# Storing split weights once per stage, and copying both halves of a PSUM bank on ScalarE, in a float32 decoder trunk

## Chip, cores and metric

The kernel runs on one core of a Trainium2 chip. The metric is the device time of one execution in microseconds (us). The engines are named as the profile names them: PE (TensorE), DVE (VectorE), ACT (ScalarE), POOL (GpSimd), and SP (SyncE), whose queue issues nearly all DMAs of this kernel.

## What is computed

A residual stream of 2048 positions by 1024 channels passes two layers, each a mixer followed by a gated per-layer embedding, and a final RMS norm:

```
for i in range(2):
    hn = rms_norm(h, norm_g[i])
    m  = swa_sink_mixer(hn, ...) if i == 0 else rwkv7_mixer(hn, ...)
    h  = h + m
    h  = h + sigmoid(h @ ple_w_gate[i]) * (p[i] @ ple_w_proj[i])
return rms_norm(h, final_norm_g)
```

The first mixer is windowed attention with sinks (16 heads of 64, window 128). The second is RWKV-7: for every head a 64 by 64 state S runs through the 2048 positions,

```
sa = einsum('bhvk,bhk->bhv', S, -kk_t)
S  = S * d_t + outer(sa, kk_t * a_t) + outer(v_t, k_t)
y  = einsum('bhvk,bhk->bhv', S, r_t)
```

and its output is normed, gated with silu(z) and multiplied by `rwkv_w_out`. Everything is float32.

## The kernel before

Activations lie transposed, channels on partitions, in 4 groups `n` of 512 positions (`G`). A float32 product is made of three matmuls in a rounded format: each operand is split into a high part (the rounded value) and a low part (the rest), and `mm3` (L565 to L569) issues high*high, high*low and low*high for each 128 by 128 block of the weight. `split` (L510 to L518) makes the high part on ACT (L516, or L513 with a scale) and the low part on DVE or POOL (L518, or L514 with a scale).

There are four phases: the attention projections (to about 500 us), attention, the RWKV projections (about 1230 to 2000 us), and the RWKV recurrence (to the end). In the second and the fourth a `Dense` object runs beside the main work: it holds a list of jobs (`kind`, `n`), a kind being a weight matrix: `p0`, `p1` or `p` (per-layer projection), `o` (output projection), `g` (gate), `l` (low rank), `z` (RWKV gate projection). A job has 8 units (2 for the projections and for `l`), a unit is 8 steps, and a step is one `mm3`, so 24 matmuls a unit. The main work calls `tick` between its own instructions, and each tick advances Dense by a step. In the attention phase the jobs are p0 for four groups, p1 for two, then `o0 g0 o1 l0 g1 o2 l1 g2 o3 l2 g3`, p1 once more and `l3`; in the recurrence z for four groups, then `o g` for three groups and `p o g` for the last. That makes 86 and 98 units.

`Dense.run` writes the order out by hand. The weight of unit `u` is loaded (`w_load`, L110 to L118) at step 8(u-2), split (`w_split`, L120 to L123) at step 8(u-1)+4 and used from step 8u. So a kind's weights are loaded and split again for every group. The raw tile, the high part `dwh` and the low part `dwl` are 4 KB a partition each and come from one pool of six such slots (`wp`, tag `w4`). A raw load reads 512 KB, in rows of 512 bytes (2 KB for the projections). All loads and stores here are issued by SP, in order. A compiler pass then sets the order of the instructions on each engine; an engine runs its own list strictly in order.

The recurrence works in 32 chunks of 64 positions. `chain` (L1301 to L1336) computes one chunk: the products `r1p`, then `up`, whose two halves of 64 partitions are copied out of one PSUM bank into `uv` (L1320 by DVE, L1321 by ACT), then the state update `sp`, `st` (DVE, L1328), the next chunk's `uv` (DVE, L1331), and the output `y`. `tri` (L1231 to L1285) inverts the triangular matrices that `chain` needs, for four chunks at a time: a recursion of 60 small DVE operations (L1247, L1249), three DVE transposes, and for each chunk two sets of 32 by 32 products in a bank `wq`. Of each, one quarter of the partitions is copied out by ACT and one by DVE (L1272 to `wt`, L1282 to `tt`). `front` prepares a chunk (`aps`, `am`, `bn`), and `output` norms and gates it.

Of the kernel before, what the change touches and what calls it, by code (L numbers as in the profile page):

```python
# [10 lines left out]
F32R = mybir.dt.float32r  # L11
# [7 lines left out]
KT = C // 128  # L19
# [24 lines left out]
def f32(ap):  # L44
    return ap.bitcast(F32)
# [7 lines left out]
class Dense:  # L53
# [54 lines left out]
        return aux  # L108

    def w_load(self, u):  # L110
        kind, n, c = u
        k = self.kinds[kind]
        kt = k.get("kt", KT)
        m = 128 * KT // kt
        raw = self.tr.wp.tile([128, KT * 128], F32, name="wraw", tag="w4")
        w = k["w"][:, k.get("c0", 0) + c * m:k.get("c0", 0) + (c + 1) * m]
        self.nc.sync.dma_start(out=raw.rearrange("p (k m) -> p k m", m=m), in_=w.rearrange("(k p) m -> p k m", p=128))
        return raw  # L118

    def w_split(self, u, raw):  # L120
        hi, lo = (self.tr.wp.tile([128, KT * 128], F32R, name=nm, tag="w4") for nm in ("dwh", "dwl"))
        self.tr.split(hi, lo, raw, scale=self.kinds[u[0]].get("scale"))
        return hi, lo  # L123

    def run(self):
        units, begin, events = [], {}, {}

        def at(step, *what):
            events.setdefault(step, []).append(what)

        owner = []
        for j, (kind, n) in enumerate(self.jobs):
            kt = self.kinds[kind].get("kt", KT)
            b = begin[kind, n] = 8 * len(units)
            units += [(kind, n, c) for c in range(self.kinds[kind].get("units", kt))]
            for k in range(kt):
                free = owner[len(owner) - KT] if len(owner) >= KT else -99
                if "after" in self.kinds[kind]:

                    fill = max(free + 1, begin[self.kinds[kind]["after"], n] + 8 * k + 8)  # L140
                else:
                    fill = max(free, b + k - 9) + 3
                    pre = 3 if "pre" in self.kinds[kind] else 0
                    if pre:
                        at(fill - pre, "pre", j, k)
                    at(fill - pre - self.lead, "fetch", j, k)
                assert fill <= b + k
                at(fill, "fill", j, k)
                if (kind, n) == self.late:
                    at(max(fill, b), "late", j, k)  # L150
                owner.append(8 * len(units) - kt + k)
        for u in range(len(units)):
            at(8 * (u - 2), "w_load", u, None)
            at(8 * (u - 1) + 4, "w_split", u, None)
            for ct in range(KT if "aux" in self.kinds[units[u][0]] and not units[u][2] else 0):
                at(8 * (u + ct) - 4, "aux", units[u][:2], ct)
        raws, tiles, wraw, ws, auxs = {}, {}, {}, {}, {}
        job = -1
        first = -16
        assert first <= min(events)  # L160
        yield
        for s in range(first, 8 * len(units)):
            self.left = 8 * len(units) - s
            for what, a, k in sorted(events.pop(s, []), key=lambda e: ("fetch", "w_load", "fill", "pre", "aux", "w_split", "late").index(e[0])):
                if what == "fetch":
                    kind, n = self.jobs[a]
                    kd = self.kinds[kind]
                    while not kd.get("ready", lambda n, k: True)(n, k):
                        yield
                    raws[a, k] = kd["fetch"](n, k)  # L170
                elif what == "fill":
                    kind, n = self.jobs[a]
                    tiles[a, k] = self.kinds[kind].get("fill", self.fill)(n, k, raws.pop((a, k), None))
                elif what == "pre":
                    kind, n = self.jobs[a]
                    raws[a, k] = self.kinds[kind]["pre"](n, k, raws[a, k])
                elif what == "aux":
                    auxs[a, k] = self.kinds[a[0]]["aux"](a[1], k)
                elif what == "late":
                    while self.rest is None:  # L180
                        yield
                    self.tr.split(*(x[:, G - self.rest.shape[2]:] for x in tiles[a, k]), self.rest[:, k])
                elif what == "w_load":
                    wraw[a] = self.w_load(units[a])
                else:
                    ws[a] = self.w_split(units[a], wraw.pop(a))
            if s >= 0:
                u, i = divmod(s, 8)
                kind, n, c = units[u]
                kd = self.kinds[kind]  # L190
                kt = kd.get("kt", KT)
                k, ct = i % kt, c * (KT // kt) + i // kt
                if k == 0:
                    if ct == 0:
                        job += 1
                    ps = self.mp.tile([128, G], F32, name="ps")
                hi, lo = ws[u]
                m = KT // kt * 128
                sl = slice(k * m + (ct % (KT // kt)) * 128, k * m + (ct % (KT // kt)) * 128 + 128)
                self.tr.mm3(ps, hi[:, sl], lo[:, sl], *tiles[job, k], k == 0, k == kt - 1)  # L200
                if k == kt - 1:
                    self.tr.start(kd["evac"](n, ct, ps, tiles[job, ct] if kt == KT else None, auxs.pop(((kind, n), ct), None)))
                    self.cols_done[kind, n] = ct + 1
            yield
# [225 lines left out]
class Trunk:  # L430
# [712 lines left out]
    def rwkv(self):  # L1143
        nc, ins = self.nc, self.ins
# [8 lines left out]
        with ExitStack() as es:  # L1153
# [28 lines left out]
            half = (slice(0, 64), slice(64, 128))  # L1182
# [48 lines left out]
            def tri(g):  # L1231
# [12 lines left out]
                for r in range(30, 0, -1):  # L1244
                    n = 31 - r
                    t = tmp[:, 0:r * n].rearrange("u (s t) -> u s t", t=n)
# [5 lines left out]
                tt = ttp.tile([128, NP, TG, LC], F32, name="tt")  # L1252
# [9 lines left out]
                for j in range(TG):  # L1262
                    wt = sm.tile([128, NP, 32], F32, name="wt")
                    wq = p_f.tile([128, 2, NP, 32], F32, name="wq", tag="f")
                    for p in range(NP):
                        for e in range(2):
                            r0 = 64 * e
                            nc.tensor.matmul(wq[r0 + 32:r0 + 64, 0, p], lhsT=ag[r0:r0 + 32, p, j, 32:64], rhs=at[r0:r0 + 32, p, j],
                                             start=True, stop=True)
                    for e in range(2):  # L1270
                        cpy = nc.vector.tensor_copy if e else nc.scalar.copy
                        cpy(wt[64 * e + 32:64 * e + 64], wq[64 * e + 32:64 * e + 64, 0])  # L1272
                    yield
                    yield
                    for p in range(NP):
                        for e in range(2):
                            r0 = 64 * e
                            nc.tensor.matmul(wq[r0:r0 + 32, 1, p], lhsT=wt[r0 + 32:r0 + 64, p], rhs=tt[r0 + 32:r0 + 64, p, j, 32:64],
                                             start=True, stop=True)
                    for e in range(2):  # L1280
                        cpy = nc.vector.tensor_copy if e else nc.scalar.copy
                        cpy(tt[64 * e:64 * e + 32, :, j, 32:64], wq[64 * e:64 * e + 32, 1])  # L1282
                    TT[g * TG + j] = tt[:, :, j]
                    yield
                if (g + 1) * TG < NCH:  # L1285
# [15 lines left out]
            def chain(c):  # L1301
                uv, am, tt, bn, xa = UV.pop(c), AM.pop(c), TT.pop(c), BN.pop(c), XA.pop(c)[:, :, :, c % 2]
# [14 lines left out]
                up = p_c.tile([128, NP, 64], F32, name="up", tag="ch")  # L1317
                for p, eo in pairs:
                    mm(up[half[eo], p], lhsT=tt[half[eo], p], rhs=r1[half[eo], p], start=True, stop=True)
                nc.vector.tensor_copy(uv[half[0], 0], up[half[0]])  # L1320
                nc.scalar.copy(uv[half[1], 1], up[half[1]])  # L1321
                self.ticks(STEPS[2])
                if c + 1 < NCH:
                    sp = p_c.tile([128, NP, 64], F32, name="sp", tag="ch")
# [2 lines left out]
                    t = r2.tile([128, NP, 64], F32, name="st")  # L1327
# [52 lines left out]
            load_front(0)  # L1380
            load_ab(0)
            self.start(tri(0))
            self.start(front(0))
            load_front(1)
# [48 lines left out]
```

## Time and profile before

| what | value |
|---|---|
| median of 3 runs | 3120.83 us (3119.34 to 3126.83) |
| profiled execution, its own time | 3124.84 us |
| its span, first to last instruction | 3123.0 us |
| granted PE clock, mean | 0.961 of full speed |
| PE busy | 2885.0 us (92%) |
| DVE busy | 2112.2 us (68%) |
| ACT busy | 1438.3 us (46%) |
| DMA moved | 532.87 MB |

All durations that stand in rows come from the one profiled execution. Its own time is 1.8 us above its span and 4.0 us above the median of the runs. A row of the windows view gives a stretch, its length, the busy time and instruction count of each engine, then the granted PE clock as a share of full speed (2.4 GHz; the lower level is 1.2 GHz), the busy share of the 16 DMA engines, and GB/s.

### The profile page before, as it was taken

Reading aid. Unit: us, or ns where it says so; the run is one execution under the profiler, and the core shown is the slowest. Engines: PE = TensorE matmul, PEld = TensorE weight load, DVE = VectorE, ACT = ScalarE, POOL = GpSimd, SP = SyncE. Lnnn points to the kernel's source line nnn. Section 1 sums busy time; section 2 is a strip of 40 time slices with the busy share of each in tenths; the row PEclk is TensorE's granted clock in tenths of the full one; section 3 lists DMA queues with packets and bytes.
Section 4 is the critical chain, followed back from the end, with each engine's and each line's share of the span. In section 5 each row is a group of like instructions: output and inputs, shape, how many; then the busy total and the mean of one; then the engine's idle time right before and its main releaser. Section 6 shows DMA issues by size and latency. Waiting matters only on the chain. (4 is left out here: it accounts for less than half of the span.)

```text
span 3123.0 us, 56427 instructions
## 1 busy us (share of the span) xinstructions
PE 2885.0 (92%) x21416; PEld 2284.2 (73%) x21416; DVE 2112.2 (68%) x3665; ACT 1438.3 (46%) x2976; POOL 1023.5 (33%) x886
## 2 busy tenths in 40 slices
PE   7999998999999988898999899988989988989997
PEld 5888886777777766686777688766767766767876
DVE  6532434775888766738678966688795686795555
ACT  5311115874675644626667733433334443443433
POOL 2243500002211232404556700214454435435421
PEclk9999999999999999999999899998899999999999
DMA  7665847985675455636556778855657558568463
GB/s 220 184 142 110 172 131 207 248 210 151 170 189 143 145 172 172 194 115 190 180 185 199 214 210 218 236 150 145 145 150 176 126 143 202 116 150 204 122 192 95
DMA packets 704032, 532.87 MB, mean 171 GB/s; under 512 B 255504, under 2 KB 558736, under 8 KB 703760
## 3 DMA queue, kind: packets, MB, share of 16 engines
q1 hardware_dynamic: 696080, 518.76, 60.3%
q0 software_dynamic: 7680, 10.50, 3.1%
q8 instruction: 169, 2.77, 0.4%
q14 instruction: 103, 0.84, 0.1%
HBM read 350.09 MB, written 168.56 MB: 166 GB/s over the span
## 5 line engine op out<-in xcount | busy, mean ns | idle before, releaser
L567 PE MATMUL ps<-dhi,dwh 128*128 128x512 f32 x1472 | 609.8, 416 | 17.0 <-ACT dwh L516 11.7
L569 PE MATMUL ps<-dhi,dwl 128*128 128x512 f32 x1472 | 595.2, 405 | 26.7 <-DVE dwl L518 15.0
L568 PE MATMUL ps<-dlo,dwh 128*128 128x512 f32 x1472 | 594.3, 405 | 8.3 <-DVE dlo L518 6.1
L567 PE MATMUL ps<-xH,wh 128*128 128x512 f32 x1408 | 556.9, 402 | 25.4 <-DVE kb L1049 10.5
L568 PE MATMUL ps<-xL,wh 128*128 128x512 f32 x1408 | 560.7, 399 | 1.8 <-DVE xL L518 1.1
L569 PE MATMUL ps<-xH,wl 128*128 128x512 f32 x1408 | 561.5, 399 | 0.8 <-DVE wl L518 0.8
L569 PEld LDWEIGHTS ps<-dhi,dwl 128*128 128x128 f32 x1472 | 283.2, 192 | 96.0 <-DVE dwl L518 18.9
L567 PEld LDWEIGHTS ps<-dhi,dwh 128*128 128x128 f32 x1472 | 283.0, 192 | 88.1 <-ACT dwh L516 12.7
L567 PEld LDWEIGHTS ps<-xH,wh 128*128 128x128 f32 x1408 | 269.4, 192 | 88.9 <-DVE kb L1049 14.0
L568 PEld LDWEIGHTS ps<-dlo,dwh 128*128 128x128 f32 x1472 | 283.5, 193 | 67.8 <-DVE dlo L518 8.4
L568 PEld LDWEIGHTS ps<-xL,wh 128*128 128x128 f32 x1408 | 270.8, 192 | 62.3 <-DVE xL L518 2.3
L569 PEld LDWEIGHTS ps<-xH,wl 128*128 128x128 f32 x1408 | 269.9, 192 | 59.3 <-DVE wl L518 1.7
L518 DVE TENSOR_TENSOR dwl<-wraw,dwh 128x1024 fp32r<-128x1024 f32 x152 | 193.8, 1275 | 106.4 <-ACT dwh L516 99.9
L516 ACT ACTIVATE dwh<-wraw 128x1024 fp32r<-128x1024 f32 x152 | 160.5, 1057 | 195.8 <-PE ps L568 122.4
L677 POOL DMA_DIRECT2D t<-t x160 | 126.2, 1272 | 200.2 <-DVE t L674 107.1
L851 ACT ACTIVATE S<-S,nm 128x256 f32<-128x256 f32 (+1 forms) x256 | 125.6, 494 | 65.5 <-DVE nm L848 60.1
L516 ACT ACTIVATE wh<-wr 128x1024 fp32r<-128x1024 f32 x44 | 46.6, 1060 | 188.3 <-DMA wr<-in_attn_w_in 142.9
L518 POOL TENSOR_TENSOR xL<-xs,xH 128x512 fp32r<-128x512 f32 x72 | 111.1, 1554 | 67.7 <-ACT xH L516 67.0
L1247 DVE TENSOR_TENSOR tmp<-P 128x30 f32<-128x30 f32 (+14 forms) x240 | 114.1, 476 | 11.2 <-POOL P L1238 5.2
L842 DVE CUSTOM_DVE_ANT_0 S<-sc,mask,sink 128x256 f32<-128x256 f32 (+1 forms) x256 | 109.0, 469 | 17.6 <-PE sc L838 17.5
L953 DVE SCALAR_TENSOR_TENSOR xs<-hp,mu,xs 128x512 f32<-128x512 f32 x96 | 95.3, 1004 | 29.5 <-ACT xs L952 29.1
L1249 DVE TENSOR_TENSOR P<-P,tmp 128x30 f32<-128x30 f32 (+14 forms) x240 | 110.1, 459 | 6.5
(258 smaller groups left out, 5341.6 us busy)
## 6 DMA issues: line engine op xcount, KB each, us to landing
wraw<-in_ple_w_gate SPq DMA_DIRECT2D x64, 512.0 KB, 4.3
hp<-hn SPq DMA_DIRECT2D x72, 256.5 KB, 4.0
sz<-th SPq DMA_DIRECT2D x64, 256.0 KB, 4.3
ple<-pt SPq DMA_DIRECT2D x64, 256.0 KB, 5.9
wraw<-in_attn_w_out SPq DMA_DIRECT2D x32, 512.0 KB, 4.4
aux<-ple SPq DMA_DIRECT2D x64, 256.0 KB, 3.9
yd<-kx SPq DMA_DIRECT2D x32, 512.0 KB, 4.5
wraw<-in_rwkv_w_in SPq DMA_DIRECT2D x32, 512.0 KB, 4.8
```

What stands on the lines that cost most here:

```text
L516: nc.scalar.activation(hi, src, AF.Copy)
L518: e.tensor_tensor(out=lo, in0=src, in1=f32(hi), op=ALU.subtract)
L567: mm(ps, lhsT=wh, rhs=ah, start=first, stop=False)
L568: mm(ps, lhsT=wh, rhs=al, start=False, stop=False)
L569: mm(ps, lhsT=wl, rhs=ah, start=False, stop=last)
L677: nc.gpsimd.dma_start(out=t1[32 * d:32 * d + 32, :], in_=t2[32 * a:32 * a + 32, :], accum_op=ALU.add)
L842: nc.vector.tensor_tensor_reduce(out=S[:, i, c0:], in0=sc[:, eo, c0:], in1=mask[:, c0:], scale=1.0, scalar=sink[:, 4 * g + 2 * j + eo:4 * ...
L851: nc.scalar.activation(S[:, i, c0:], S[:, i, c0:], AF.Exp, bias=nm[:, i:i + 1], accum_out=den[:, i:i + 1])
L953: nc.vector.scalar_tensor_tensor(out=src, in0=t[:, :G], scalar=mus[:, c, k:k + 1], in1=src, op0=ALU.mult, op1=ALU.add)
L1247: nc.vector.tensor_tensor(out=t, in0=P[:, 0:r, r:r + 1].broadcast_to([128, r, n]), in1=P[:, r:r + 1, r + 1:].broadcast_to([128, r, n]), op ...
L1249: nc.vector.tensor_tensor(out=P[:, 0:r, r + 1:], in0=P[:, 0:r, r + 1:], in1=t, op=ALU.add)
```

## The change

There are two edits.

First, `Dense.run` notes for every kind the group of its first job (`first`) and whether it comes again (`again`). A unit of the first group is loaded and split as before; if the kind comes again, the two parts are also stored to a scratch tensor in DRAM (`parts`, 2 by 512 KB for a unit). A unit of a later group loads both parts from there into two slots (`w_parts`), at the step at which it loaded the raw weight, and nothing is split. The rows of these transfers are 4 KB, one a partition.

Second, the copies at L1272, L1282, L1320 and L1321 are all made by ACT.

```
     def w_load(self, u):
         kind, n, c = u
         k = self.kinds[kind]
+        if n != self.first[kind]:
+            return self.w_parts(u)
...
+    def w_parts(self, u):
+        hl = tuple(self.tr.wp.tile([128, KT * 128], F32R, name=nm, tag="w4") for nm in ("dwh", "dwl"))
+        for a, t in enumerate(hl):
+            self.nc.sync.dma_start(out=f32(t), in_=self.parts(u)[a])
+        return hl
+
+    def parts(self, u):
+        return self.tr.dram(f"wp_{self.name}{u[0]}{u[2]}", [2, 128, KT * 128])
+
     def w_split(self, u, raw):
+        if u[1] != self.first[u[0]]:
+            return raw
         hi, lo = (self.tr.wp.tile([128, KT * 128], F32R, name=nm, tag="w4") for nm in ("dwh", "dwl"))
         self.tr.split(hi, lo, raw, scale=self.kinds[u[0]].get("scale"))
+        if self.again[u[0]]:
+            for a, t in enumerate((hi, lo)):
+                self.nc.sync.dma_start(out=self.parts(u)[a], in_=f32(t))
         return hi, lo

     def run(self):
         units, begin, events = [], {}, {}
+        self.first, self.again = {}, {}
+        for kind, n in self.jobs:
+            self.again[kind] = kind in self.first
+            self.first.setdefault(kind, n)
...
                     for e in range(2):
-                        cpy = nc.vector.tensor_copy if e else nc.scalar.copy
-                        cpy(wt[64 * e + 32:64 * e + 64], wq[64 * e + 32:64 * e + 64, 0])
+                        nc.scalar.copy(wt[64 * e + 32:64 * e + 64], wq[64 * e + 32:64 * e + 64, 0])
...
                     for e in range(2):
-                        cpy = nc.vector.tensor_copy if e else nc.scalar.copy
-                        cpy(tt[64 * e:64 * e + 32, :, j, 32:64], wq[64 * e:64 * e + 32, 1])
+                        nc.scalar.copy(tt[64 * e:64 * e + 32, :, j, 32:64], wq[64 * e:64 * e + 32, 1])
...
-                nc.vector.tensor_copy(uv[half[0], 0], up[half[0]])
-                nc.scalar.copy(uv[half[1], 1], up[half[1]])
+                for eo in range(2):
+                    nc.scalar.copy(uv[half[eo], eo], up[half[eo]])
```

## Rows read from the trace of the kernel before

**Rows 1.** The page: busy time of each engine, and PE's granted clock in 40 slices.
```profile
PE 2885.0 (92%) x21416; PEld 2284.2 (73%) x21416; DVE 2112.2 (68%) x3665; ACT 1438.3 (46%) x2976; POOL 1023.5 (33%) x886
PEclk9999999999999999999999899998899999999999
```

**Rows 2.** Windows: the recurrence, one of eight stretches in it, all eight summed.
```profile
2050.00:3000.00 950.00, 857.79 (x11156) 680.96 (x11155) 715.55 (x1078) 384.52 (x801) 428.57 (x350) 0.95 0.63 152
...
2100.00:2170.00 70.00, 57.66 (x749) 45.92 (x743) 68.13 (x105) 23.60 (x41) 38.88 (x32) 0.88 0.42 106
...
sum 410.00, PE 340.35 PEld 268.93 DVE 395.93 ACT 143.76 POOL 177.66; mean PE 42.54 PEld 33.62 DVE 49.49 ACT 17.97 POOL 22.21
```

**Rows 3.** Waits of PE, 2050 to 3123 us: us in total, times, longest.
```profile
PE y L1334 <- DVE uv L1320: 15.6, 7, 4.9
...
PE ps L569 <- DVE dwl L514: 11.7, 4, 4.9
PE aps L1208 <- DVE tt L1282: 10.1, 4, 3.3
PE ps L569 <- DVE dwl L518: 8.0, 5, 3.3
```

**Rows 4.** Timeline of 2136 to 2152 us: start, us, engine, line, [idle before <-releaser].
```profile
2138.35 0.52 PE L1319 MATMUL up<-r,tt 64*64 64x64 f32 x12
...
2142.16 2.06 DVE L518 TENSOR_TENSOR dwl<-wraw,dwh 128x1024 fp32r<-128x1024 f32 x1
...
2144.27 0.50 PE L569 MATMUL ps<-dhi,dwl 128*128 128x512 f32 x1 [3.33 <-DVE dwl L518]
...
2146.31 0.67 DVE L1320 COPY uv<-up 64x512 f32<-64x512 f32 x1
...
2147.02 0.58 ACT L1321 COPY uv<-up 64x512 f32<-64x512 f32 x1 [9.24 <-DVE uv L1320]
```

**Rows 5.** Costliest groups: weight splits of all phases; then the scaled ones, from 2050 us.
```profile
L518 DVE TENSOR_TENSOR dwl<-wraw,dwh 128x1024 fp32r<-128x1024 f32 x152 | 193.8, 1275 | 106.4 <-ACT dwh L516 99.9
L516 ACT ACTIVATE dwh<-wraw 128x1024 fp32r<-128x1024 f32 x152 | 160.5, 1057 | 195.8 <-PE ps L568 122.4
...
L514 DVE SCALAR_TENSOR_TENSOR dwl<-wraw,dwh 128x1024 fp32r<-128x1024 f32 x32 | 41.8, 1305 | 12.1 <-ACT dwh L513 11.9 <-DMA uv<-vn 0.2
```

**Rows 6.** Single lines: copies with ns min/median/max; last, one of ACT's waits, 2050 to 3050 us.
```profile
L1272 DVE COPY wt<-wq x32: 429/429/432, 2077.2 to 2865.6; 32x256 f32<-32x256 f32 x32
...
L1282 ACT COPY tt<-wq x32: 343/362/362, 2082.2 to 2870.1; 32x256 f32<-32x256 f32 x32
...
L1320 DVE COPY uv<-up x32: 646/679/683, 2089.8 to 2973.8; 64x512 f32<-64x512 f32 x32
...
L1321 ACT COPY uv<-up x32: 581/581/583, 2090.6 to 2974.5; 64x512 f32<-64x512 f32 x32
...
ACT uv L1321 <- DVE uv L1320: 121.7, 28, 14.3
```

**Rows 7.** The eight stretches, instructions of `dwl` alone (PE, PEld, DVE); last, L1320 alone.
```profile
2400.00:2440.00 40.00, 11.48 (x30) 5.60 (x29) 3.66 (x3) 0.96 0.52 116
2510.00:2570.00 60.00, 14.84 (x36) 6.87 (x36) 6.12 (x5) 0.97 0.60 141
...
sum 410.00, PE 98.11 PEld 46.42 DVE 37.80; mean PE 12.26 PEld 5.80 DVE 4.73
...
sum 410.00, DVE 8.78; mean DVE 1.10
```

**Rows 8.** DMA issues: count, KB each, median us to landing; then a window of dense work alone.
```profile
wraw<-in_ple_w_gate SPq DMA_DIRECT2D x64, 512.0 KB, 4.3
...
yd<-kx SPq DMA_DIRECT2D x32, 512.0 KB, 4.5
...
3020.00:3090.00 70.00, 68.45 (x300) 54.80 (x299) 34.64 (x41) 24.97 (x58) 6.48 (x4) 1.00 0.41 125
```

**Rows 9.** Line L117, the weight loads: their time to landing, min/median/max.
```profile
DMA to landing us min/median/max: 3.5/4.6/13.4
```

## Prediction

> **What bounds the kernel now.** I read the page's busy times first. PE is busy 92% of the span, DVE 68%, ACT 46% [rows 1]. The change leaves the matmuls alone, so it can give back only the time in which PE stands still (3123.0 - 2885.0 = 238 us) and the time in which it runs at the lower clock. The 40 slices show where the clock falls: at the start, around 550, 650, 1100 to 1500, 1750, and again and again after 2050 us. The next view is therefore the windows of the recurrence. From 2050 to 3000 us PE is idle 950 - 857.8 = 92.2 us, and the mean clock is 0.95 [rows 2]. Eight stretches of 20 to 70 us, 410 us together, hold 410 - 340.4 = 69.7 us of these 92; in them DVE is busy 395.9 us, that is 97% [rows 2]. These are the stretches in which the recursion of `tri` runs. So in 43% of this phase DVE is the bound, and PE the bound in the rest.
>
> Third, the waits of PE say which DVE results are late: `uv` of L1320 15.6 us, `dwl` of L514 11.7 and of L518 8.0, `tt` of L1282 10.1 [rows 3]. All four are instructions that the change removes from DVE, wholly or in most units; together 45.4 us.
>
> Fourth, the timeline of one such place shows how. The products `up` end about 2138.9 us. Their copy L1320 starts on DVE only at 2146.3, since DVE works off recursion steps and a 2.06 us `dwl` first; PE waits 3.33 us for that `dwl`, and ACT stands 9.24 us before its own half, L1321 [rows 4]. The last point matters: ACT's copy reads other partitions than DVE's, yet it starts only when DVE's has ended. ACT loses 121.7 us in 28 such waits [rows 6]. The program orders the two readers of one bank.
>
> **Part one: weights kept as parts.** Of 86 units in the attention phase, 22 are of a first group (p0 2, p1 2, o 8, g 8, l 2), and of 98 in the recurrence 26 (z 8, p 2, o 8, g 8). So 136 units lose their split. 24 of these are scaled ones (o in the recurrence, groups 1 to 3), 112 are plain. DVE loses 112 x 1.275 + 24 x 1.305 = 174 us and ACT 136 x 1.057 = 144 us [rows 5].
>
> Outside the DVE-bound stretches this lies beside PE work and is worth nothing but the waits it ends. In the eight stretches `dwl` costs DVE 37.8 us. Two of them are first passes, which keep their split: 2400 to 2440 is o0 (3.7 us), 2510 to 2570 nearly all g0 (6.1) [rows 7]. That leaves 28.0 us that DVE loses where it is the bound.
>
> What is added: 136 x 2 = 272 loads for 136, and 46 units of the first groups that come again (22 + 24; p of the recurrence is used once) store 2 x 512 KB each. So SP issues 228 more DMAs, and 136 x 0.52 + 46 x 1.05 = 119 MB more are moved. One transfer of 512 KB lands in the same time whether its rows are 512 bytes (the gate's weights, 4.3 us) or 4 KB (yd, a store of the very shape of a part, 4.5 us) [rows 8]. In a window of dense work alone the DMA engines move 125 GB/s at a busy share of 0.41, so about 305 GB/s at full share [rows 8]; 119 MB is then an estimate of 390 us of their time, 12% of the span. It is hidden where their share is below 0.85; the mean in the recurrence is 0.63 [rows 2].
>
> Is a part there in time? A part's slot comes free with the last matmul of unit u-3, and unit u begins two units later: 48 matmuls. In the window of dense work PE did 300 in 68.45 us, so 48 take 11.0 us at the least, against 4.6 us to landing in the median and 13.4 at worst [rows 8, 9]. The stores wait on SP for the split of their own unit; behind them on SP stand the loads of the next chunk and of the next weights. The loads of raw weights wait there today for the same splits, so I take the queue at nothing, with up to +13 us for one full landing [rows 9] that a crowded start of the attention phase may push onto PE. I take +3: nearer to nothing, since two p0 units are stored before the crowd.
>
> One cost sits in the slots. Where a first-group unit is followed by a later-group one, the pool of six must hold the running unit's two, the raw tile, the next unit's two parts loaded early, and two more for the split: seven. The low part waits for the running unit's last matmul. There are seven such places (after p0, p1, g0, l0 in the attention phase; after z0, o0 g0, and the late p). The price is between 0 and one ACT and one DVE split, 1.06 + 1.28 = 2.3 us [rows 5]: 0 to 16 us together. I take +4, since the high part still finds a slot and PE needs the low part only in a unit's third matmul.
>
> **Part two: copies on ACT.** DVE loses 32 x 0.679 = 21.7 us (L1320), 32 x 0.429 = 13.7 (L1272) and about as much at L1282; ACT gains 32 x (0.581 + 2 x 0.362) = 42 us [rows 6], less than the 144 us it loses. In the eight stretches it is L1320 that counts, 8.8 us [rows 7]. On the chain itself the two halves take 0.68 + 0.58 = 1.26 us one after the other today and 2 x 0.58 = 1.16 on ACT: nothing. The gain is that no half waits behind the recursion. What is queued behind them on ACT are `dwh`, `am` and `th`; they stood 121.7 us behind L1321 and now wait for 0.58 us more of work.
>
> The Trainium skill speaks against this edit: "PSUM — Partial Sum Buffer", section "PSUM bank collisions raise a hardware error", says that two engines may read one bank at once when they are in different 32-partition quadrants, as these halves are. Had the copies run so, one engine for both would add 32 x 0.58 = 18.6 us to the chain, and the sum below would be some 27 us instead of 46. The trace does not show them so: in rows 4 ACT's copy stands behind DVE's, after 9.24 us of waiting; the sum goes by the row.
>
> **The sum.** (a) DVE-bound stretches: 28.0 + 8.8 = 36.8 us less DVE work, under the 69.7 us that PE is idle there, so -36.8. (b) Outside them, `tt` of L1282: between 0 and -10.1 [rows 3]; -6, because ACT has room. (c) The clock: 950 x 0.05 = 47.5 us of work lost at most [rows 2], between 0 and all of it. It falls behind PE's idle time, and (a) and (b) take nearly half of that, but in a DVE-bound stretch a faster PE only waits longer; -10. (d) slots +4, (e) DMA +3. Sum -45.8 us. From the profiled execution's 3124.84 us this gives 3079.0; against the median of 3120.83, 4.0 lower, **3075**. Its own bounds: (a) may be half as large or half as large again (18 to 55 us), (c) may reach half of the clock (24 us); together they move the sum by some 28 us either way, 3047 to 3103.
>
> **Rivals.**
>
> The relief goes deeper (chance 0.10). If three quarters of the 92.2 idle us and of the 47.5 us of clock go, 105 us, less the +7 of (d) and (e): about 3023. For it speaks that all four waits named end; against, that the recursion stays on DVE and goes on meeting POOL's work.
>
> The freed DVE time is filled again (0.17). DVE instructions are stretched when POOL works beside them: a `dwl` of 1.2 us took 2.06 in rows 4. The recursion may stretch into the room, or another late result may take the place of `dwl`. Then only the direct order gains: a quarter of (a) and (b), -11, with -3 of clock and +7: -7, about 3114. The Trainium skill has the rule for it, "SBUF — State Buffer", section "SBUF: two separate sides": DVE with two SBUF inputs and GpSimd share a port pair that one locks for its whole instruction. A `dwl` is such an instruction and its removal also frees POOL, so by the rule this rival should be weak.
>
> Weights come late (0.10, slower). The place is dense work with nothing between: the end of the attention phase and the last 16 units. The point is where a part's landing passes the 11.0 us lead. The worst landing today, 13.4 us [rows 9], would stop PE 2.4 us a unit, and with twice the bytes behind one another 4.5 us is not absurd: 16 units at the end and some 22 of the attention tail, 38 x 2.4 = 91 us at the worst, 75 as the case that decides. With the gain that is 3075 + 75 = 3150. Against it: the DMA share there is only 0.41 [rows 8].
>
> The change does what it says on the page, so a rival of no effect is the second one.
>
> **Numbers.** Forecast 0.63, deeper 0.10, filled 0.17, late 0.10. About 0.3% (9.4 us) is what a measurement of this kernel can tell from no change. Faster by more than that: nearly all of the forecast (0.61), deeper 0.10, and a part of filled (0.07), 0.78. Within it: 0.11. Slower: the late weights and an edge of others, 0.11. The range goes from 3035, into the deeper case, to 3118, over most of the filled one.
>
> **What would show it.** Right: DVE busy falls by about 220 us and ACT by about 100; 48 weight splits are left; the waits for `dwl` and L1320 nearly go; in the `tri` stretches PE's busy share rises from 83% and the clock with it; ACT no longer waits for DVE at L1321. Wrong: DVE still 97% busy over as many us (filled); PE waits for DMA of `dwh` (late); PE waits on `dwl` at the seven places for more than 2 us each (slots); a new wait behind ACT's copies. What would upset the sum most is that the compiler pass orders each engine's list anew, which the trace of before can't show.

## The result, and the profile after

The changed kernel takes **3078.73 us** (median of 4 runs, 3062.65 to 3083.21) against 3120.9 (median of 4, 3119.34 to 3126.83): a ratio of **0.985, 95% interval 0.982 to 0.988**, or 42 us. The forecast was 3075, with a range of 3035 to 3118. The total is right to 4 us; where the 42 us come from is mostly not where the forecast had them. In the experiments below, the ratios leave out two executions of the kernel before that took 5463 and 11877 us.

The profiled execution took 3082.86 us, with a span of 3081.1. First the page's busy times, and the weight splits that are left (two lines of the view of single source lines: ns min/median/max, first and last start).

```profile
PE 2863.4 (93%) x21416; PEld 2265.3 (74%) x21416; DVE 1907.0 (62%) x3433; ACT 1356.3 (44%) x2936; POOL 1002.1 (33%) x886
PEclk9999999999999999999999999998999999999999
...
DMA packets 622689, 652.42 MB, mean 212 GB/s; under 512 B 259153, under 2 KB 433361, under 8 KB 622417
...
L540 DVE TENSOR_TENSOR dwl<-wraw,dwh x40: 1180/1224/1823, 468.8 to 2962.7; 128x1024 fp32r<-128x1024 f32 x40
L536 DVE SCALAR_TENSOR_TENSOR dwl<-wraw,dwh x8: 1212/1218/1503, 2334.9 to 2424.8; 128x1024 fp32r<-128x1024 f32 x8
```

Against [rows 1], DVE loses 205 us and ACT 82. 40 plain splits are left here and 8 scaled ones on L536, 48 together. The DMAs move 119.6 MB more. The work changed as the diff says. Of the three slices with an 8 in the clock's row one is left.

Now the recurrence in the windows view, a window of the same length, 42 us earlier (columns as explained with the profile before), and then one place of the recursion in it.

```profile
2008.00:2958.00 950.00, 868.26 (x11230) 685.43 (x11230) 625.16 (x959) 379.91 (x849) 421.39 (x353) 0.95 0.76 211
...
2130.00:2180.00 50.00, 40.80 (x422) 31.94 (x419) 48.81 (x74) 17.81 (x32) 33.36 (x26) 0.83 0.64 178
...
sum 340.00, PE 288.96 PEld 229.42 DVE 322.16 ACT 113.33 POOL 146.23; mean PE 41.28 PEld 32.77 DVE 46.02 ACT 16.19 POOL 20.89
```

Against [rows 2], DVE is relieved of 90 us (715.55 to 625.16), but PE's idle time falls only from 92.2 to 81.7 us, and the clock stays at 0.95. The last line is the sum of seven stretches of 30 to 60 us in which DVE is still about 95% busy; before there were eight, 410 us long. PE is idle 51.0 us in them (69.7 before), and outside them 30.7 (22.5 before). The edges of these stretches are set by eye and the new ones are 70 us shorter in all, so the split between inside and outside is rough. The whole is not: from the first `r1p` to the last `y`, the same work in both kernels, DVE is busy 106 us less (729.1 before, 623.3 now), and PE is idle only 7.5 us less (93.0 and 85.5). PE's busy time is 869.15 us in both.

PE's waits from 2008 us to the end (us in total, times, longest) name what is late now:

```profile
PE ps L589 <- ACT dhi L538: 14.4, 7, 9.2
PE ps L421 <- DVE th L327: 14.2, 7, 7.1
PE r1p L1327 <- DVE uv L1351: 12.0, 4, 6.1
PE ps L591 <- DVE dwl L540: 11.2, 4, 6.7
PE wq L1290 <- DVE at L1277: 6.3, 1, 6.3
...
PE r1p L1327 <- POOL tt L1282: 5.1, 2, 2.7
PE ps L591 <- DVE dwl L536: 4.8, 1, 4.8
...
PE ps L591 <- DMA dwl<-wp_wo: 0.3, 1, 0.3
```

Compare [rows 3]. The wait for `uv` of L1320 (15.6 us) is gone, and there stands one for the chain's next DVE step, `uv` of L1351 (L1331 before), with 12.0. `dwl` fell from 19.7 us (11.7 and 8.0) only to 16.0, though most of its instructions are gone. At the top stands a wait that ACT seems to cause.

The timeline of that place shows what it is (start, us, engine, line, [idle before <-releaser]):

```profile
2140.93 1.76 DVE L299 SCALAR_TENSOR_TENSOR xs<-xs,mu,raw 128x512 f32<-128x512 f32 x1
2142.61 1.47 DVE L1269 TENSOR_TENSOR tmp<-P 128x220 f32<-128x220 f32 x1
...
2150.33 1.12 DVE L1269 TENSOR_TENSOR tmp<-P 128x238 f32<-128x238 f32 x1
...
2153.70 0.41 DVE L1269 TENSOR_TENSOR tmp<-P 128x238 f32<-128x238 f32 x1
...
2154.90 0.75 DVE L299 SCALAR_TENSOR_TENSOR xs<-xs,mu,raw 128x512 f32<-128x512 f32 x1
...
2155.74 0.63 ACT L538 ACTIVATE dhi<-xs 128x512 fp32r<-128x512 f32 x1 [12.33 <-DVE xs L299]
...
2156.43 0.80 PE L589 MATMUL ps<-dhi,dwh 128*128 128x512 f32 x1 [9.20 <-ACT dhi L538]
```

PE waits 9.20 us for ACT, but ACT itself waited 12.33 us for `xs`, a single DVE instruction of 0.75 us. Between this `xs` and the one before it, DVE works off 15 instructions of the recursion in one piece, 12.3 us. Nothing of what the change removed is in this piece. That is the mechanism that most of these waits share: **DVE runs its list in order, and a long piece of recursion in the list holds up whatever stands behind it.** Take out `dwl` and `uv`, and `xs`, `th` or the next `uv` stands there.

The piece is long for a second reason. Its first eight instructions, with POOL at work beside them, take 1.1 to 1.5 us each, and the later ones, with POOL idle, 0.4 us: about 5 of the 12.3 us. Over the phase this adds up. The first of the eight groups, with POOL idle beside it, needs 19.9 us of DVE for its 60 instructions; the other seven need 26 to 33. At 19.9 us for each group, an estimate, some 64 of the recursion's 223 us would go. No run takes POOL's work away, so what that is worth to PE is not shown.

**Where the 42 us arise.** The first matmul of two lines and the last of a third cut each trace in four parts: the first low-rank product `ls` ends the attention phase, the first `r1p` and the last `y` bound the recurrence. All numbers are from one profiled execution each, in us, with the difference to the kernel before.

| kernel | to first `ls` | to first `r1p` | to last `y` | to the end |
|---|---|---|---|---|
| before | 1252.8 | 765.9 | 961.9 | 142.4 |
| after | 1222.5 (-30.3) | 761.9 (-4.0) | 954.4 (-7.5) | 142.3 |
| the same again, other chip | 1221.6 (-31.2) | 755.7 (-10.2) | 943.2 (-18.7) | 142.4 |

The second part, the RWKV projections, is the same in all kernels, and yet differs by up to 10 us; differences of that size in one profile are no evidence. 30 us in the first part are: they come back, as 26 to 31, in every run that has the whole first edit there, and the three other kernels without it end that part within 5 us of the kernel before. The prediction had no gain in that part.

Two places make up most of it. In the windows view, kernel before and then after:

```profile
600.00:800.00 200.00, 194.35 (x1032) 151.57 (x1031) 137.51 (x361) 126.16 (x324) 29.52 (x20) 0.98 0.69 190
1040.00:1260.00 220.00, 198.00 (x842) 156.03 (x841) 148.46 (x184) 108.51 (x179) 67.77 (x55) 0.95 0.55 168
```

```profile
600.00:800.00 200.00, 200.00 (x1070) 156.02 (x1069) 136.19 (x369) 124.14 (x320) 32.68 (x21) 1.00 0.98 312
1040.00:1260.00 220.00, 206.15 (x881) 162.88 (x880) 126.70 (x157) 96.60 (x159) 78.34 (x68) 0.98 0.76 250
```

The first stretch loses its 5.7 us of idle time and gets the full clock; in the second 13.9 of 22.0 idle us are left and the clock rises from 0.95 to 0.98. That is 38 and 39 matmuls more in the same time. Counted by PE's matmuls, the kernel after is 2.6 us ahead where the kernel before stands at 650 us, 13.8 at 700, 11.5 at 1100 and 29.3 at 1250: about 11 us come from the first place and 18 from the tail. What stood there in the kernel before, in its timeline, first the place near 690 us and then the phase's tail:

```profile
678.62 0.73 SPq L117 DMA_DIRECT2D wraw<-in_attn_w_out  x1
...
692.12 1.06 ACT L516 ACTIVATE dwh<-wraw 128x1024 fp32r<-128x1024 f32 x1 [7.40 <-DMA wraw<-in_attn_w_out]
...
693.23 0.80 PE L567 MATMUL ps<-dhi,dwh 128*128 128x512 f32 x1 [5.03 <-ACT dwh L516]
```

```profile
1102.09 0.72 ACT L952 ACTIVATE xs<-hp,omu 128x512 f32<-128x512 f32 x1 [2.52 <-DMA hp<-hn]
1104.62 0.72 ACT L952 ACTIVATE xs<-hp,omu 128x512 f32<-128x512 f32 x1 [1.80 <-DMA hp<-hn]
...
1107.67 1.04 ACT L516 ACTIVATE dwh<-wraw 128x1024 fp32r<-128x1024 f32 x1
...
1108.77 0.80 PE L567 MATMUL ps<-dhi,dwh 128*128 128x512 f32 x1 [6.20 <-ACT dwh L516]
1111.73 0.80 PE L569 MATMUL ps<-dhi,dwl 128*128 128x512 f32 x1 [1.74 <-DVE dwl L518]
...
1127.62 0.50 PE L569 MATMUL ps<-dhi,dwl 128*128 128x512 f32 x1 [3.03 <-DVE dwl L518]
```

The load issued at 678.62 is the one that took the 13.4 us of [rows 9]; its split, and PE behind it, waited for it. This is a load of `o0`, a first group, which the kernel after loads and splits as well. So what stood here is not what the change takes out. From 670 to 695 us PE stands idle 4 to 5 us in the traces of all four kernels whose attention phase is as before, and not at all in any trace with the edit there; in the kernel after, no load of this stretch takes over 10.3 us to land. Why none comes as late as in the kernel before, among more transfers, is not shown.

In the tail it is the order again: ACT's list has the first mixes of the next phase (`xs`, L952) ahead of a weight split, and these wait for their input from DRAM, while the split's own tile is there. PE stands 6.20 us, then works at the lower of its two levels for about 6 us (0.63 us a matmul, against 0.39 ahead of the stall). These are units of later groups. In the kernel after they have nothing on ACT and DVE, so nothing of theirs can stand behind anything there.

### The profile page after: what moved, and what is told of

Read it like the earlier page. It is cut to its first block, busy times and chain, and to the rows that moved or that the text cites. A ratio compares the mean times of both kernels' runs of the same rounds, so it can differ in the third digit from the quotient of the medians.

```text
span 3081.1 us, 56458 instructions
## 1 busy us (share of the span) xinstructions
PE 2863.4 (93%) x21416; PEld 2265.3 (74%) x21416; DVE 1907.0 (62%) x3433; ACT 1356.3 (44%) x2936; POOL 1002.1 (33%) x886
## 5 line engine op out<-in xcount | busy, mean ns | idle before, releaser
L591 PE MATMUL ps<-dhi,dwl 128*128 128x512 f32 x1472 | 593.5, 404 | 16.8 <-DVE dwl L540 11.5
L1269 DVE TENSOR_TENSOR tmp<-P 128x30 f32<-128x30 f32 (+14 forms) x240 | 113.0, 471 | 16.1 <-POOL P L1260 9.7
L1052 POOL TENSOR_TENSOR kb<-kb,mhalf 128x16 f32<-128x16 f32 x32 | 100.6, 3146 | 33.8 <-DVE kb L1051 33.3
L264 DVE TENSOR_TENSOR aux<-ps,aux 128x512 f32<-128x512 f32 x64 | 43.8, 686 | 108.3 <-PE ps L591 95.7
L1233 ACT COPY am<-aps 128x512 f32<-128x512 f32 x128 | 69.5, 591 | 90.5 <-PE aps L1230 90.1
```

The source lines that it names most:

```text
L591: mm(ps, lhsT=wl, rhs=ah, start=False, stop=last)
L1052: nc.gpsimd.tensor_tensor(out=bs[:, :, 0], in0=bs[:, :, 0], in1=self.mhalf.broadcast_to([128, m]), op=ALU.pow)
L1233: nc.scalar.copy(am[:, 4 * i:4 * i + 4, eo], pse[eo])
L1269: nc.vector.tensor_tensor(out=t, in0=P[:, 0:r, r:r + 1].broadcast_to([128, r, n]), in1=P[:, r:r + 1, r + 1:].broadcast_to([128, r, n]), op ...
```

## The experiments

All ratios are against runs of the kernel before on the same chip, with their 95% interval. The table goes on with the parts of the one above.

| kernel | time, us | ratio | to `ls` | to `r1p` | to last `y` |
|---|---|---|---|---|---|
| copies_only | 3104.99 | 0.995 (0.993 to 0.997) | +1.0 | -0.6 | -17.1 |
| att_weights | 3095.93 | 0.993 (0.990 to 0.996) | -31.1 | -1.8 | +5.1 |
| rec_weights | 3095.64 | 0.993 (0.991 to 0.995) | +4.3 | -8.5 | -17.9 |
| weights_only | 3067.05 | 0.983 (0.980 to 0.986) | -28.9 | -10.2 | -16.7 |
| change_again | 3071.21 | 0.984 (0.982 to 0.987) | -31.2 | -10.2 | -18.7 |
| weights_uv | 3069.93 | 0.984 (0.982 to 0.986) | -28.9 | -7.9 | -22.5 |
| no_recursion | 3003.07 | 0.963 (0.960 to 0.965) | -29.4 | -6.4 | -84.7 |
| slow_recursion | 3052.16 | 0.979 (0.976 to 0.981) | -30.2 | -4.1 | -39.5 |
| att_last_group | 3114.55 | 0.9984 (0.9974 to 0.9995) | -14.8 | -0.6 | +3.1 |
| before_slow | 3121.29 | 1.000 (0.999 to 1.001) | +1.2 | -8.9 | +0.4 |
| weights_slow | 3070.01 | 0.985 (0.981 to 0.989) | -26.2 | -7.0 | -23.4 |
| early_slow | 3088.61 | 0.990 (0.988 to 0.992) | -29.6 | -8.8 | +13.6 |

**The second edit alone** (copies_only): the kernel before with the four copies on ACT.

```diff
-                nc.vector.tensor_copy(uv[half[0], 0], up[half[0]])
-                nc.scalar.copy(uv[half[1], 1], up[half[1]])
+                for eo in range(2):
+                    nc.scalar.copy(uv[half[eo], eo], up[half[eo]])
```

(and the same for `wt` and `tt`.)

> The kernel before with the copies at L1272, L1282, L1320 and L1321 on ScalarE; weights as before. First theory (the prediction's: VectorE's room in the stretches of the recursion is what counts): about 9 us of VectorE work leave those stretches and the wait for uv of L1320 ends, so 9 to 15 us faster, all of it after 2000 us. Second theory (from the two traces: the attention phase gave most of the gain, by weights no longer split behind other work): 0 to 5 us faster, since VectorE takes up the room again. Both: nothing changes before 2000 us beyond 3 us.

Measured: 14 us faster, 17 in the recurrence of its profile. PE's and ACT's waits from 2010 us on:

```profile
PE r1p L1305 <- DVE uv L1329: 27.1, 8, 6.2
...
ACT uv L1319 <- PE up L1317: 20.3, 20, 1.6
```

ACT's wait for DVE (121.7 us, [rows 6]) is gone, and so is PE's for the copy (15.6 us, [rows 3]). The chain's next DVE instruction has taken it over with 27.1 (4.6 in the kernel before). Both halves on one engine did not make the kernel longer. The rule of the Trainium skill that the prediction weighed ("PSUM — Partial Sum Buffer", section "PSUM bank collisions raise a hardware error": engines in different quadrants may read a bank at once) would by the prediction's estimate have put 18.6 us onto the chain; in this kernel the program orders the two copies, and the measurement decides. The two copies share the bank that they read and also the tile that they write; which of the two makes the program order them, no run shows.

**The first edit in one phase only** (att_weights, rec_weights): `kept` takes the place of the test on `first`.

```diff
+    def kept(self, kind, n):
+        return n != self.first[kind] and (self.name == "a")
```

(in rec_weights the name is "w".)

> The change's first edit in the attention phase alone (weights of the recurrence are split for every group as before, and no copy is moved). First theory: between +7 and -5 us, as the sum had it (slots and DMA cost about what the end of the phase gains). Second theory: 25 to 32 us faster, 11 of them near 690 us and 18 between 1090 and 1230 us, where the kernel before waits for weight splits; PE's waits for dwh and dwl between 600 and 1250 us go from about 16 us to under 3.

> The change's first edit in the recurrence alone, no copy moved. First theory: 28 us of splits leave the stretches in which VectorE is busy 97%, with some of the clock 30 to 38 us faster. Second theory: at most 10 us faster; PE's idle time in the 950 us of the recurrence falls from 92 us to no less than 80, and waits for other VectorE results take the place of those for dwl.

Measured: 23 us faster with either. In att_weights the whole gain stands ahead of the first `ls` (-31.1), as in the change; the recurrence gives none of it (+5.1, within what single profiles differ by). So the attention phase is worth 23 to 31 us by itself, though PE was 90% busy there and more. In rec_weights the first part shows no gain, and the recurrence gains 18, with `PE y <- DVE uv` still at 15.9 us. So neither phase alone is the cause; the prediction's place is half of it at the most.

**The first edit alone, and the change again** (weights_only, change_again).

> The change's first edit in both phases, no copy moved. First theory: 37 us of the 46, so about 3084 us. Second theory: the sum of the two phases, 30 to 40 us faster. If the parts add up, this is att_weights and rec_weights together within 5 us, and the changed kernel less copies_only.

> The changed kernel itself, beside runs of the kernel before on this chip, so that it can be set beside the parts. The earlier runs give 0.985 for it and 0.983 for its first edit alone; the two edits alone took 13.6 and 51.6 us. If the edits added up it would be 65 us faster than before, 0.979; if both only empty the same queue, 40 to 50 us, 0.984 to 0.987.

The first edit alone is 52 us faster; its two phases alone gave 23 each, 46 together, so within the intervals they add. The change is 49 us faster in its second measurement, 42 in its first. So the copies do not add: worth 14 us alone, they are worth nothing that can be measured beside the weights (0.984 and 0.985 with them, 0.983 without). PE's waits in weights_only from 1980 us:

```profile
PE y L1356 <- DVE uv L1342: 16.1, 7, 5.2
PE ps L591 <- DVE dwl L540: 14.5, 5, 6.4
```

The wait for the copy is there as before (16.1 us), so it is no longer worth its own size: what ends it brings up another wait. The runs of the change spread from 3062.65 to 3083.21 us over both measurements; the two profiles differ mostly in the recurrence, 954.4 against 943.2 us.

**Only the copy of the chain** (weights_uv): the first edit, and of the copies only `uv` on ACT.

> The first edit in both phases, and of the copies only L1320 (uv) on ScalarE; wt and tt as before. If the uv copy is what counts of the second edit (PE waits 16 us for it in the first edit alone), this is 10 to 16 us faster than the first edit alone, 0.978 to 0.980. If the wait only moves on to the next VectorE step of the chain (L1331, uv of the next chunk) it is within 6 us of the first edit alone, and PE's wait for that step rises from 2.5 us to over 10.

3069.93 us, the same as weights_only. The wait for the copy goes, and this one comes:

```profile
PE r1p L1329 <- DVE uv L1353: 10.0, 4, 3.9
```

It was 2.5 us in weights_only. The wait moved one DVE instruction on along the chain. The other two copies (`wt`, `tt`) are not what spends the gain.

**Taking the recursion away** (no_recursion): the change, with the last 2 of the 30 recursion steps; 56 of the 60 DVE instructions of a group are left out, so the inverse is not computed.

```diff
-                for r in range(30, 0, -1):
+                for r in range(2, 0, -1):
```

> The changed kernel with the triangular recursion cut to its last two of 30 steps (56 of 60 VectorE operations of each of the 8 groups left out, some 205 us of VectorE work in all; the inverses are not formed). If the recursion's run of VectorE work is what holds PE in the recurrence, PE's idle time between 2000 and 2960 us falls from 82 to under 35 us, and the kernel is 50 us or more faster than the changed one. If the stops come from elsewhere (the chain's own latency, PSUM, DMA), PE stays idle for over 60 us and less than 25 us are gained.

The recurrence loses 85 us against before, 66 to 77 more than the change. The windows of the recurrence, this kernel and then change_again:

```profile
1980.00:2940.00 960.00, 927.86 (x11586) 736.44 (x11587) 477.86 (x562) 396.30 (x880) 445.92 (x366) 0.97 0.83 234
```

```profile
1980.00:2940.00 960.00, 876.88 (x11329) 691.32 (x11327) 637.63 (x988) 384.11 (x855) 423.23 (x356) 0.96 0.77 215
```

PE's idle time falls from 83 to 32 us. Everything else is in place: the weights' DMAs, the copies, the chain. So in the changed kernel the recursion on DVE is what holds PE in this phase. The kernel before was not run without it. Leaving the recursion out also makes the inverse ready sooner, but PE's waits for the inverse itself are small in the list of the kernel after: 6.3 us for `at` and 5.1 for `tt`, of 85.5 idle. Most of the waits there are for other results on DVE or behind it.

**Spreading the recursion** (slow_recursion): the change, and in the program the recursion gives way to other work after every step instead of every second. No work is left out.

```diff
-                    if r % 2:
-                        yield
+                    yield
```

> The changed kernel with one yield after every step of the recursion instead of after every second, so that its 60 VectorE operations are spread over twice as many ticks of the main loop (same work). If it is the density of these runs that makes PE wait, VectorE's stretches over 95% get thinner and the kernel is 10 to 30 us faster than the changed one. If the compiler's order packs them anyway, or the inverse now comes late to its chunk, it is within 6 us or slower.

**3052.16 us** (3049.64 to 3058.74), ratio 0.979 (0.976 to 0.981): 19 us faster than the change on the same chip and 68 than the kernel before, the best of those that form the inverse. PE's waits from 1980 us:

```profile
PE ps L591 <- DVE dwl L540: 15.7, 4, 7.2
PE ps L421 <- DVE th L327: 9.6, 8, 3.4
```

The chain's wait for `uv` is down to 1.9 us, from 9.9 in change_again. But the trace does not show the recursion in shorter pieces. In DVE's timeline 19 pieces of it run for over 5 us with no other instruction between, 138 us together; in change_again there are 17, 130 us together. From first to last instruction the eight groups take 295 us instead of 327, with fewer other instructions between, and 209 us of DVE instead of 225. The largest difference is in the third group, here the stretch around it in change_again and then in slow_recursion:

```profile
2114.00:2166.00 52.00, 42.04 (x426) 32.16 (x425) 50.09 (x84) 17.33 (x32) 32.90 (x28) 0.84 0.59 161
```

```profile
2138.00:2175.00 37.00, 37.00 (x437) 29.15 (x437) 33.54 (x74) 14.36 (x25) 12.84 (x12) 0.96 0.73 199
```

The group fits into 37 us instead of 52, with 13 us of POOL's work beside it instead of 33, and PE does not stand still. So the compiler's pass packed the recursion more densely, where the edit asked for the opposite; both forms of the expectation are missed. The edit is worth 19 us; that it is so because less of POOL's work falls beside the recursion fits these rows, but no run shows it.

**What the spreading needs** (before_slow, weights_slow, early_slow). The same edit in the kernel before; in weights_only; and, one step further, a yield after each of the two instructions of a step, with `tri` begun up to one chunk earlier.

> The kernel before with one yield after every step of the recursion; neither edit. If the packing of the recursion is a bound of its own, this is 15 to 25 us faster than before, as it was on the changed kernel. If it only pays when the splits are gone (VectorE is 75% busy here against 66%), under 8 us.

> The first edit in both phases, copies as before, and the recursion spread as in slow_recursion. If the second edit is worth nothing beside the first, this equals slow_recursion (0.9785) within 0.003. If the copies count once the recursion no longer fills VectorE, this is 8 us or more slower than slow_recursion.

> The changed kernel with the recursion spread still more: a yield after each of its 60 operations, and the inverse for the next four chunks begun as soon as the one before is done. If thinner is better, 10 to 25 us faster than slow_recursion (3052 us). If the gain of spreading is used up, within 8 us; if the inverse now comes late, slower than it.

In the kernel before it is worth nothing (1.000, 0.999 to 1.001). In weights_only it is worth nothing that can be measured either (0.985 after 0.983). With both edits it is worth 19 us. PE's largest wait in weights_slow, and then in before_slow, is for the copy that DVE still makes there:

```profile
PE y L1355 <- DVE uv L1341: 31.2, 10, 6.0
```

```profile
PE y L1333 <- DVE uv L1319: 27.9, 11, 4.3
```

Without the extra `yield` it was 16.1 us (weights_only) and 15.6 (before). So the copies do pay, by some 18 us (3070.01 against 3052.16, two intervals that barely part), but only with the list that the extra `yield` brings: on DVE the copy waits longer there, on ACT it does not. early_slow gains only 31 us; its recurrence is 13.6 us longer than that of the kernel before, though its recursion too takes only 210 us of DVE. It changes the spacing and the start together, and which of the two does it wasn't tried.

**Which places in the attention phase** (att_last_group): the first edit in the attention phase, for the jobs of the last group only. The splits in the tail go; those near 690 us stay.

```diff
+    def kept(self, kind, n):
+        return n != self.first[kind] and (self.name == "a" and n == NG - 1)
```

> The first edit in the attention phase alone and there only for the jobs of the last group (o3, g3, l3 load stored parts; all others are split as before). If the gain between 1090 and 1230 us comes from weight splits that stood on ScalarE and VectorE behind the next phase's work, it is here in full: 15 to 20 us faster, and the place near 690 us gives nothing. If it comes from less of VectorE's work over the whole phase, 5 us or less.

Its profile is 15 us ahead at the first `ls`, and the three waits of the tail shown above are gone. Counted by matmuls, it gains 19 us on the kernel before between 1100 and 1250 us, all that the change gains there, but stands 8 us behind at 1100. The median gains only 5 us (0.9974 to 0.9995): the recurrence of the profile loses 3, and the rest lies within what single profiles differ by. It didn't tell the two places apart, either: the stall near 690 us is absent here too, though its loads are raw as before (PE is busy 199.13 us from 600 to 800). The whole order of the lists is laid out anew when jobs change. So that the tail's waits came from splits behind the next phase's mixes is shown. That the place near 690 us goes with the edit is shown too, and by the count of matmuls it is about 11 of the 30 us; which of the moved loads and stores does it stays open.

## Why the prediction was right, and where it was wrong

**What it had right.** 48 splits left, DVE -205 (said: about -220) and ACT -82 (about -100). 119.6 MB more moved (119). ACT no longer waits for DVE at L1321. The parts are never late: PE's only wait for a part's DMA is 0.3 us, so the slower rival (3150) is excluded, even where the DMA share reached 0.98. Term (e), +3, can't be told from these waits alone: beside these 0.3 us, PE's waits for ACT's `dwh` in the recurrence rose from 0.4 to 8.7 us, the longest of them (3.6) behind a raw load that took 9.3 us to land; that the stores of parts ahead of it made it slow is not shown.

**Term (a), -36.8 us, was too large.** Its step was that DVE work taken out of a DVE-bound stretch comes off PE's idle time one for one. Over the whole recurrence DVE lost 106 us of work and PE 7.5 us of idle time; PE's share in the stretches of the recursion rose only from 83% to 85%. The step fails because DVE's list is in order: what PE waits for is the place of one instruction in it, not the sum of DVE's work. When `dwl` and `uv` were out, `xs` and `th` stood behind the same recursion. Each edit alone gave 17 to 18 us in the recurrence, and both together 8 to 19 in the profiles: the two parts of (a) were added, and in the medians too the copies add nothing to the weights.

**Term (b), -6, went to another wait.** The 10.1 us for L1282 ended; `r1p` now waits 5.1 for the same tile's memset on POOL and `wq` 6.3 for the transpose L1277.

**Term (c), -10, was nothing.** The clock of the phase is 0.95 before and after. It falls behind PE's stalls, and these stayed.

**Term (d), +4, was wrong in kind.** PE's list above has 16.0 us in five waits for `dwl`, three of them over 2 us. Over the whole recurrence, its start included, PE waited 25.0 us for `dwl` and `dwh`, about as much as before (22.3), though 26 splits are left there of 98. So the sign "the waits for `dwl` nearly go" failed. The longest, in the timeline of after:

```profile
2955.36 7.26 DVE L444 TENSOR_TENSOR res<-res,rs 128x512 f32<-128x512 f32 x6 [1.12 <-POOL rs L439]
...
2962.67 1.21 DVE L540 TENSOR_TENSOR dwl<-wraw,dwh 128x1024 fp32r<-128x1024 f32 x1
...
2963.94 0.79 PE L591 MATMUL ps<-dhi,dwl 128*128 128x512 f32 x1 [6.74 <-DVE dwl L540]
```

It is not a slot that is late but the split's place behind 7.26 us of the output's norm; the raw unit in question is the late `p`. The other four stand behind steps of the recursion or its three transposes (6 us) on DVE. The price there is not one split's length (2.3 us, the prediction's upper bound) but what stands ahead of it on DVE.

**The term that was missing is the largest: about -30 us in the attention phase.** The prediction said that outside the DVE-bound stretches the splits are "worth nothing but the waits it ends", read the waits from 2050 us on, and so looked up none in the attention phase. The list of PE's waits from 600 to 1260 us in the kernel before names 16 us of them (`dwh`, `dwl`; 5.0 of it at `o0`, whose splits stay), and 6.1 for a weight `wh` of the next phase, whose split stands in the same lists; in the kernel after none of the three is left:

```profile
PE ps L567 <- ACT dwh L516: 11.2, 2, 6.2
PE ps L567 <- ACT wh L516: 6.1, 1, 6.1
PE ps L569 <- DVE dwl L518: 4.8, 2, 3.0
```

with the work at the lower clock behind them. The prediction's first paragraph named a lower clock around 650 and from 1100 us, and didn't follow it.

So the forecast's total was right by luck, by two errors of about the same size: in the recurrence it promised 53 us and the change gave 8 to 19, and in the attention phase it charged up to 7 and the change gave 30. The rival "filled again" holds for the recurrence, in the form that another late result takes the place; its other form, that the recursion stretches into the room, does not. The page's lines of its two instructions in the kernel before and after:

```profile
L1247 DVE TENSOR_TENSOR tmp<-P 128x30 f32<-128x30 f32 (+14 forms) x240 | 114.1, 476 | 11.2 <-POOL P L1238 5.2
L1249 DVE TENSOR_TENSOR P<-P,tmp 128x30 f32<-128x30 f32 (+14 forms) x240 | 110.1, 459 | 6.5
```

```profile
L1269 DVE TENSOR_TENSOR tmp<-P 128x30 f32<-128x30 f32 (+14 forms) x240 | 113.0, 471 | 16.1 <-POOL P L1260 9.7
L1271 DVE TENSOR_TENSOR P<-P,tmp 128x30 f32<-128x30 f32 (+14 forms) x240 | 110.4, 460 | 6.9
```

224.2 us before, 223.4 after.

## What to carry to other kernels

Taking work off a busy in-order engine gains only up to the next late result on the same list, and two edits that empty the same queue don't add; look for the long piece of work that everything waits behind. One `yield` in it was worth 19 us, but only with both edits, and the trace shows a list that is packed more densely, not one that is broken up: where a compiler lays out the lists, read the new list before you say why an edit paid. For a change that acts in several phases, list the waits of every phase by the lines that it removes, also of those in which the engine looks 90% busy. A right total is no proof of the terms: cut the trace at milestones and set each term against its own part.

## What the runs showed of the hardware

- The DMA engines held a busy share of 0.98 and 312 GB/s over 200 us (600 to 800 in the kernel after), and PE did not stand still in them. The prediction's estimate of 305 GB/s at full share fits.
- A recursion step on DVE takes about three times as long beside POOL: 1.12 us with 238 elements at 2150.33, while POOL's `xs` runs until 2151.19, and 0.41 us for the same instruction at 2153.70, after it. That such a lock exists is the rule of the Trainium skill that the prediction cited ("SBUF — State Buffer", section "SBUF: two separate sides"); its size in this kernel is from the trace.
- Runs of one kernel spread by about 10 us either way where the recurrence is held by DVE (3062.65 to 3083.21 for the change), and by 1.5 us in the only two without the recursion.
